# A quarter of the first residual pair on ScalarE's DMA queue, at the front of its program

## The chip, the cores and the metric

One core of a Trainium2 chip. The metric is the device time of one execution in microseconds (us), as a median over fast executions. Profiles are single executions of the same kernels; their span, from first to last instruction, is about 1.8 us shorter than the device time. DMA engines are the 16 engines that move data between memory (HBM) and the core's on-chip memory (SBUF); in these traces a packet is one row of a transfer on one of them (before: 3,072 packets of 16 KB, 128 of the weights' 1,152 bytes, 304 of 4 bytes for the semaphores).

## The reference

A 3x3 convolution with padding 1 over 16 images of 64 channels, 64x64 pixels, plus a residual of the output's shape, all float32:

```python
x        = randn(16, 64, 64, 64)
weight   = randn(64, 64, 3, 3) * 0.1
residual = randn(16, 64, 64, 64)
output[b, co] += weight[co, ci, kh, kw] * x_pad[b, ci, kh:kh+64, kw:kw+64]   # over ci, kh, kw
return output + residual
```

x and residual are read and the output written once: three times 16.8 MB, about 50.5 MB with the weights.

## The kernel before

Images go in pairs: 2 x 64 channels fill the 128 partitions, one image is a row of 4,096 floats (16 KB) per partition. x has three buffers; the residual has one tile `ro` for all eight pairs, into which VectorE adds the convolution from PSUM (TensorE's result memory) and which is then stored. All transfers are issued by SyncE, on one queue, in program order: x pair 0 (moved ahead of the entry barrier, where the engines wait for one another at the start; ScalarE's first recorded instruction comes at 0.96 us), the weights, residual pair 0, x pair 1, residual pair 1, x pair 2, then the rest as buffers come free.

```python
NPIX = H * W                                    # 4096
RES = (slice(0, 1), slice(1, 2), slice(2, 4), slice(4, 6), slice(6, 8))
res_bc = residual.rearrange("(p b) c h w -> (b c) p (h w)", b=2)
...
def load_x(p):
    return nc.sync.dma_start(out=xr[p % NXR][:, :], in_=x_bc[128 * p : 128 * p + 128, :]).then_inc(s_x[p % NXR], 16)

def load_ro(i):
    if i >= 2:
        nc.sync.wait_ge(s_r[i % 2], 16 * (i // 2))
    nc.sync.dma_start(out=ro[:, RES[i], :], in_=res_bc[:, RES[i], :]).then_inc(s_r[i % 2], 16)
...
def to_the_front(dma):       # moves the issue ahead of the first Drain of its engine, before the entry barrier
    ...
for p in range(NPAIR):
    if p >= NXR:
        nc.sync.wait_ge(s_half, 2 * (p - NXR) + 3)
    if p == 0:
        to_the_front(load_x(p))
        nc.sync.dma_start(out=wraw[:, :], in_=w_rows[:, :]).then_inc(s_w, 16)
    else:
        load_x(p)
    if p in (0, 1, 3, 5, 7):
        load_ro((p + 1) // 2)
for k in range(NEARLY):                         # stores of pairs 0-1, 2-3, 4-5; 6 and 7 follow at the end
    nc.sync.wait_ge(s_add, 4 * k + 5)
    store(slice(2 * k, 2 * k + 2)).then_inc(s_out, 16)
```

ScalarE casts x to bfloat16, TensorE transposes the weights once and then runs 384 matmuls, VectorE adds.

Of the kernel before, what the change touches and what calls it, by code (L numbers as in the profile page):

```python
# [15 lines left out]
def kernel(  # L16
# [7 lines left out]
    nc = tc.nc  # L24
# [6 lines left out]
    NPIX = H * W  # L31
# [4 lines left out]
    NXR = 3  # L36
    NXP = 4
    NZERO = 4 + 2 * NXP
    NEARLY = 3
    RES = (slice(0, 1), slice(1, 2), slice(2, 4), slice(4, 6), slice(6, 8))  # L40

    res_bc = residual.rearrange("(p b) c h w -> (b c) p (h w)", b=2)
# [8 lines left out]
    ro = pool.tile([128, NPAIR, NPIX], FP32)  # L51
# [10 lines left out]
    s_r = [sem(f"s_r{i}") for i in range(2)]  # L62
# [8 lines left out]
    def load_x(p):  # L71
        return nc.sync.dma_start(out=xr[p % NXR][:, :], in_=x_bc[128 * p : 128 * p + 128, :]).then_inc(s_x[p % NXR], 16)

    def load_ro(i):
        if i >= 2:
            nc.sync.wait_ge(s_r[i % 2], 16 * (i // 2))
        nc.sync.dma_start(out=ro[:, RES[i], :], in_=res_bc[:, RES[i], :]).then_inc(s_r[i % 2], 16)

    def store(pairs):
        return nc.sync.dma_start(out=out_bc[:, pairs, :], in_=ro[:, pairs, :])  # L80
# [21 lines left out]
    def to_the_front(dma):  # L102



        def fixed(ap):
            t = ap.bass_ap.tensor.name
            return mybir.PhysicalAccessPattern(
                ap=ap.ap, offset=ap.bass_ap.offset, dtype=ap.dtype, memref=t, memsetref=t + "_set", bass_ap=ap.bass_ap
            )  # L110

        front = nc.main_func.blocks[0].instructions
        here = nc.cur_bb.bb.instructions
        ins = here.pop()
        assert ins.name == dma.ins.name
        at = next(
            i for i, e in enumerate(front) if e.engine == ins.engine and isinstance(e, mybir.InstDrain)
        )
        front.insert(at, copy.replace(ins, ins=[fixed(a) for a in ins.ins], outs=[fixed(a) for a in ins.outs]))
# [5 lines left out]
    def weight_block(h, half, d, par, kh):  # L125

        at = 64 * half + 32 * h
        return dict(out=wl[at : at + 32, d, :, par, :], in_=tp[0:32, kh, 0:384].rearrange("p (kw co h) -> p kw co h", kw=3, h=2)[:, :, :, h])

    with tc.tile_critical(no_gpsimd_drain=True):  # L130
# [7 lines that stand above are left out]
                nc.sync.dma_start(out=wraw[:, :], in_=w_rows[:, :]).then_inc(s_w, 16)  # L138
            else:
                load_x(p)  # L140
            if p in (0, 1, 3, 5, 7):
                load_ro((p + 1) // 2)
        for k in range(NEARLY):
            nc.sync.wait_ge(s_add, 4 * k + 5)
            store(slice(2 * k, 2 * k + 2)).then_inc(s_out, 16)


        nc.gpsimd.memset(ident[:, :], 0.0).then_inc(s_id, 1)  # L148
        nc.gpsimd.wait_ge(s_id, 1)
        nc.gpsimd.affine_select(  # L150
            out=ident[:, :],
            in_=ident[:, :],
            compare_op=mybir.AluOpType.not_equal,
            fill=1.0,
            base=0,
            pattern=[[-1, 128]],
            channel_multiplier=1,
        ).then_inc(s_id, 1)
        nc.gpsimd.wait_ge(s_id, 2)
        for t in xp:  # L160
            nc.gpsimd.memset(t[0:64, 0, :], 0.0).then_inc(s_id, 1)  # L161
            nc.gpsimd.memset(t[64:128, J, :], 0.0).then_inc(s_id, 1)  # L162
        nc.gpsimd.memset(wl[0:64, 0, :, 1, :], 0.0).then_inc(s_id, 1)  # L163
        nc.gpsimd.memset(wl[64:128, 1, :, 0, :], 0.0).then_inc(s_id, 1)  # L164


        for n in range(B):
            p, im = divmod(n, 2)
            hp = slice(64 * im, 64 * im + 64)
            x4 = xr[p % NXR].rearrange("q (j two w) -> q j two w", two=2, w=W)  # L170
            t = xp[n % NXP]
            if im == 0:
                nc.scalar.wait_ge(s_x[p % NXR], 16 * (p // NXR + 1))
            i = nc.scalar.copy(out=t[64:128, 0:J, :], in_=x4[hp, :, 0, :])  # L174
            i.then_inc(s_half, 1)
            if n >= NXP:
                i._wait_ge(s_conv, n - NXP + 1)
            nc.scalar.copy(out=t[0:64, 1 : J + 1, :], in_=x4[hp, :, 1, :]).then_inc(s_pack, 1)  # L178
            if n == 0:
                nc.scalar.wait_ge(s_id, NZERO + 1)  # L180
                for b in blocks[4:]:
                    for h in range(2):
                        i = nc.scalar.copy(**weight_block(h, *b))  # L183
                i.then_inc(s_id, 1)


        nc.vector.wait_ge(s_id, NZERO + 1)
        for k, b in enumerate(blocks[:4]):
            for h in range(2):
                i = nc.vector.tensor_copy(**weight_block(h, *b))  # L190
                if k == h == 0:
                    i.then_inc(s_bank, 2)
        i.then_inc(s_id, 1)
        for n in range(B):
            p, im = divmod(n, 2)
            hp = slice(64 * im, 64 * im + 64)
            o4 = ro[:, p, :].rearrange("q (j two w) -> q j two w", two=2, w=W)
            psj = ps[n % 2].rearrange("q c j w -> q (c j) w")
            if im == 0:
                i = next(i for i, pairs in enumerate(RES) if p < pairs.stop)  # L200
                nc.vector.wait_ge(s_r[i % 2], 16 * (i // 2 + 1))
            for par in range(2):
                i = nc.vector.tensor_tensor(  # L203
                    out=o4[hp, :, par, :], in0=psj[64 * par : 64 * par + 64, :, :], in1=o4[hp, :, par, :], op=ADD
                )
                if par == 0:
                    i._wait_ge(s_conv, n + 1)

                i.then_inc(s_add if par == 0 or n == B - 1 else s_bank, 1)


        nc.tensor.wait_ge(s_id, NZERO)
        nc.tensor.wait_ge(s_w, 16)
        wraw3 = wraw.rearrange("p (ci t) -> p ci t", t=9)
        for t in range(9):
            i = nc.tensor.transpose(  # L216
                out=tp[0:32, t // 3, 128 * (t % 3) : 128 * (t % 3) + 128], in_=wraw3[:, :, t], identity=ident[:, :]
            )
        i.then_inc(s_id, 1)
        nc.tensor.wait_ge(s_id, NZERO + 3)  # L220
        with nc.Fori(0, B // NXP, 1, engines=[PE]):
            for n in range(NXP):
                nc.tensor.wait_ge(s_bank, 1).then_inc(s_bank, -1)
                nc.tensor.wait_ge(s_pack, 1).then_inc(s_pack, -1)  # L224
                order = [(1, 0), (1, 1), (0, 0), (0, 1), (2, 0), (2, 1)]
                for i, (kw, d) in enumerate(order):
                    xlo, xhi = max(0, 1 - kw), min(W, W + 1 - kw)
                    for c in range(NCHUNK):
                        j0 = JC * c
                        m = matmul(  # L230
                            ps[n % 2][:, c, :, xlo:xhi],
                            wl[:, d, kw, :, :].rearrange("q r c -> q (r c)"),
                            xp[n][:, j0 + d : j0 + d + JC, xlo + kw - 1 : xhi + kw - 1],
                            i == 0,
                            i == len(order) - 1,
                            c == 0,
                        )
                m.then_inc(s_conv, 1)


    for p in range(2 * NEARLY, NPAIR):
        store(slice(p, p + 1))
    with tc.tile_critical(sync_engine=mybir.EngineType.Pool, no_gpsimd_drain=True):
        nc.gpsimd.wait_ge(s_out, 16 * NEARLY)
        tc.free_semaphores([s_w, *s_x, *s_r, s_out, s_id, s_half, s_pack, s_bank, s_conv, s_add])
# [30 lines left out]
```

## Time and profile before

| | before |
|---|---|
| median time | 122.76 us (3 runs, 122.63 to 122.86) |
| span of the profiled run | 120.8 us |
| first data packet, last data packet | 1.007 us, 119.61 us |
| last addition of VectorE ends | 104.3 us |

### The profile page before, as it was taken

What the parts mean: (1) busy time and instruction counts of PE and PEld (TensorE: products, weight loads), DVE (VectorE), ACT (ScalarE), POOL (GpSimd) and SP (SyncE); (2) the same over time, 40 slices, a digit from 0 to 9 for tenths busy, and PEclk for the clock granted to TensorE, in tenths of its full rate; (3) what the DMA queues carried; (4) which work ended last, traced back from release to release, by engine and by line L of the source; (5) the groups of instructions that cost most, each with busy time, mean ns of one, the idle gap of its engine ahead of it and who ended that gap; (6) DMA issues with size and microseconds to landing.
All of it is one profiled execution on the core that took longest, in us unless ns stands there. A gap on an engine that the chain in (4) does not pass through costs nothing.

```text
span 120.8 us, 734 instructions
## 1 busy us (share of the span) xinstructions
PE 87.9 (73%) x393; PEld 10.7 (9%) x105; DVE 76.0 (63%) x40; ACT 63.1 (52%) x37; POOL 2.4 (2%) x16
## 2 busy tenths in 40 slices
PE   0024499999999999999999999999999990000000
PEld 0011001101010011011111111011111100000000
DVE  0005400789898988989879898988989879500000
ACT  4049959948999923999960999883000000000000
POOL 5200000000000000000000000000000000000000
PEclk9999999999999999999999999999999999855555
DMA  7999999999999999999999999999999999999994
GB/s 168 428 428 428 428 428 434 428 434 434 428 434 434 434 428 434 434 434 434 434 434 423 423 428 434 423 412 434 434 434 434 423 434 434 434 428 434 434 434 174
DMA packets 3504, 50.48 MB, mean 418 GB/s; under 512 B 304, under 2 KB 432, under 8 KB 432
## 3 DMA queue, kind: packets, MB, share of 16 engines
q1 hardware_dynamic: 3504, 50.48, 98.5%
HBM read 33.70 MB, written 16.78 MB: 418 GB/s over the span
## 4 chain that ended last, share of the span: by engine, by line
PE 71%; DVEq 2%; DVE 2%; issue 0%
PE ps L87 53%; PE ps L86 18%; DVEq L130 2%; DVE ro L203 2%
## 5 line engine op out<-in xcount | busy, mean ns | idle before, releaser
L203 DVE TENSOR_TENSOR ro<-ps,ro 64x2048 f32<-64x2048 f32 x32 | 73.2, 2289 | 17.7 <-PE ps L87 17.2
L87 PE MATMUL ps<-xp,wl 128*128 128x504 bf16 (+1 forms) x288 | 80.0, 388 | 0.0
L86 PE MATMUL ps<-xp,wl 128*128 128x504 bf16 (+1 forms) x96 | 37.4, 389 | 3.4 <-PEq L224 3.4
L174 ACT CAST xp<-xr 64x2048 bf16<-64x2048 f32 x16 | 30.3, 1896 | 18.3 <-DMA xr<-in_x_dram 17.2
L178 ACT CAST xp<-xr 64x2048 bf16<-64x2048 f32 x16 | 30.4, 1897 | 0.4
L86 PEld LDWEIGHTS ps<-xp,wl 128*128 128x128 bf16 x96 | 9.5, 99 | 79.1 <-issue 79.1
L190 DVE CAST wl<-ps 32x192 bf16<-32x192 f32 x8 | 2.8, 348 | 10.6 <-PE ps L216 10.5
L216 PE MATMUL ps<-ident,wraw 128*32 128x128 f32 x9 | 2.1, 413 | 8.3 <-DMA wraw<-in_weight_dram 8.3
L216 PEld LDWEIGHTS ps<-ident,wraw 128*32 128x32 f32 x9 | 1.2, 137 | 8.7 <-issue 8.2
L174 ACT ACT_TABLE_LOAD x1 | 1.3, 1283 | 1.0 <-SPq L130 1.0
L183 ACT CAST wl<-ps 32x192 bf16<-32x192 f32 x4 | 1.2, 306 | 0.0
L162 POOL MEMSET xp<- 64x64 bf16 x4 | 0.6, 147 | 0.2
L161 POOL MEMSET xp<- 64x64 bf16 x4 | 0.6, 145 | 0.2
L150 POOL TENSOR_SCALAR_AFFINE_SELECT ident<-ident 128x128 f32<-128x128 f32 x1 | 0.3, 294 | 0.2 <-POOL ident L148 0.2
L164 POOL MEMSET wl<- 64x192 bf16 x1 | 0.3, 253 | 0.1
L163 POOL MEMSET wl<- 64x192 bf16 x1 | 0.3, 252 | 0.1
L148 POOL MEMSET ident<- 128x128 f32 x1 | 0.2, 205 | 0.6 <-SPq L130 0.6
L260 POOL MEMSET const-bfloat16-1.0<- 128x1 bf16 x1 | 0.1, 112 | 0.0
L260 POOL MEMSET const-uint8-127<- 128x1 uint8 x1 | 0.1, 112 | 0.0
L260 POOL MEMSET const-float32-0.0<- 128x1 f32 x1 | 0.1, 105 | 0.2 <-issue 0.2
L260 POOL MEMSET const-float32-1.0<- 128x1 f32 x1 | 0.1, 109 | 0.0
## 6 DMA issues: line engine op xcount, KB each, us to landing
xr<-in_x_dram SPq DMA_DIRECT2D x8, 2048.0 KB, 15.3
ro<-in_residual_dram SPq DMA_DIRECT2D x3, 4096.0 KB, 24.0
out_dram<-ro SPq DMA_DIRECT2D x3, 4096.0 KB, 33.2
ro<-in_residual_dram SPq DMA_DIRECT2D x2, 2048.0 KB, 15.9
out_dram<-ro SPq DMA_DIRECT2D x2, 2048.0 KB, 12.8
wraw<-in_weight_dram SPq DMA_DIRECT2D x1, 144.0 KB, 7.1
```

Of the source, the lines that this page charges most:

```text
L86: return e.matmul(out=out_, lhsT=lhsT, rhs=rhs, start=start, stop=stop, skip_group_check=True)
L87: return e.add_instruction(mybir.InstMatmult(name=nc.get_next_instruction_name(), engine=PE, ins=[e.lower_ap(rhs), e.lower_ap(lhsT)], outs ...
L130: with tc.tile_critical(no_gpsimd_drain=True):
L161: nc.gpsimd.memset(t[0:64, 0, :], 0.0).then_inc(s_id, 1)
L162: nc.gpsimd.memset(t[64:128, J, :], 0.0).then_inc(s_id, 1)
L174: i = nc.scalar.copy(out=t[64:128, 0:J, :], in_=x4[hp, :, 0, :])
L178: nc.scalar.copy(out=t[0:64, 1 : J + 1, :], in_=x4[hp, :, 1, :]).then_inc(s_pack, 1)
L183: i = nc.scalar.copy(**weight_block(h, *b))
L190: i = nc.vector.tensor_copy(**weight_block(h, *b))
L203: i = nc.vector.tensor_tensor(out=o4[hp, :, par, :], in0=psj[64 * par : 64 * par + 64, :, :], in1=o4[hp, :, par, :], op=ADD)
L216: i = nc.tensor.transpose(out=tp[0:32, t // 3, 128 * (t % 3) : 128 * (t % 3) + 128], in_=wraw3[:, :, t], identity=ident[:, :])
L260: nc = _bacc.Bacc("TRN2", target_bir_lowering=False, num_devices=1)
```

## The change

The intent is to use a hole at the very start: SyncE's queue begins slowly (885 KB from 1 to 4 us, where the plateau's rate would give 1,287), so a second queue gets work at once. A quarter of the columns of residual pair 0 (4 KB of each 16 KB row, 0.5 MB) is issued by ScalarE ahead of the entry barrier. SyncE's issue at the old place brings the other 12 KB of each row. The semaphore's counts rise by 16.

```diff
+    R0 = NPIX // 4
...
-    def load_ro(i):
+    def load_ro(i, e=nc.sync, cols=slice(0, NPIX)):
         if i >= 2:
-            nc.sync.wait_ge(s_r[i % 2], 16 * (i // 2))
-        nc.sync.dma_start(out=ro[:, RES[i], :], in_=res_bc[:, RES[i], :]).then_inc(s_r[i % 2], 16)
+            e.wait_ge(s_r[i % 2], 16 * (i // 2 + (i % 2 == 0)))
+        return e.dma_start(out=ro[:, RES[i], cols], in_=res_bc[:, RES[i], cols]).then_inc(s_r[i % 2], 16)
...
-            if p in (0, 1, 3, 5, 7):
+            if p == 0:
+                load_ro(0, cols=slice(R0, NPIX))
+            if p in (1, 3, 5, 7):
                 load_ro((p + 1) // 2)
...
+        to_the_front(load_ro(0, nc.scalar, slice(0, R0)))
...
-                nc.vector.wait_ge(s_r[i % 2], 16 * (i // 2 + 1))
+                nc.vector.wait_ge(s_r[i % 2], 16 * (i // 2 + 1 + (i % 2 == 0)))
```

## The prediction

> **What bounds the kernel now.** I read the page's first parts, then the stretches of the first and last microseconds, then the issues on SyncE's queue. The page:
>
> ```profile
> span 120.8 us, 734 instructions
> PE 87.9 (73%) x393; PEld 10.7 (9%) x105; DVE 76.0 (63%) x40; ACT 63.1 (52%) x37; POOL 2.4 (2%) x16
> ...
> DMA  7999999999999999999999999999999999999994
> GB/s 168 428 428 428 428 428 434 428 434 434 428 434 434 434 428 434 434 434 434 434 434 423 423 428 434 423 412 434 434 434 434 423 434 434 434 428 434 434 434 174
> ...
> q1 hardware_dynamic: 3504, 50.48, 98.5%
> ```
>
> No compute engine is above 73%, while one DMA queue fills the 16 DMA engines for 98.5% of the span, at 423 to 434 GB/s in nearly every slice. The chain that ended last on the page is TensorE's, but it ends with the last addition at 104.3 us; the last 15 us are stores draining. So the bound is the volume, 50.48 MB, and only two things can move the end: fewer DMA idle or slow moments, or cheaper packets. The low slices are the first and the last. The stretches of one microsecond (last two columns: DMA share and GB/s, a packet counted wholly where it starts, so single shares can pass 1):
>
> ```profile
> 0.00:1.00 1.00, 0.00 (x0) 0.00 (x0) 0.00 (x0) 0.04 (x1) 0.22 (x5) 1.00 0.00 0
> 1.00:2.00 1.00, 0.00 (x0) 0.00 (x0) 0.00 (x0) 1.00 (x1) 0.66 (x4) 1.00 1.62 295
> 2.00:3.00 1.00, 0.00 (x0) 0.00 (x0) 0.00 (x0) 0.24 (x1) 0.73 (x6) 1.00 0.58 213
> 3.00:4.00 1.00, 0.00 (x0) 0.00 (x0) 0.00 (x0) 0.00 (x0) 0.78 (x4) 1.00 0.90 377
> 4.00:5.00 1.00, 0.00 (x0) 0.00 (x0) 0.00 (x0) 0.00 (x0) 0.00 (x0) 1.00 1.07 459
> ...
> 118.00:119.00 1.00, 0.00 (x0) 0.00 (x0) 0.00 (x0) 0.00 (x0) 0.00 (x0) 0.50 1.11 475
> 119.00:120.00 1.00, 0.00 (x0) 0.00 (x0) 0.00 (x0) 0.00 (x0) 0.00 (x0) 0.50 0.05 16
> ```
>
> Nothing moves before 1.0 us, and from 1 to 4 us the DMA engines carry 295 + 213 + 377 = 885 KB where about 429 KB per microsecond would be 1,287. The trace's records of single packets say why: the 16 first packets (16 KB each, one per DMA engine) start at 1.007 to 1.275 us and last 0.72 to 2.03 us; the 82 packets that start in the first 5 us average 814 ns, all others 611 ns (the exception is 75 to 80 us, 625 ns, where loads give way to stores). The excess at the start is 82 x (814 - 611) / 16 = 1.04 us per DMA engine. After it there is no idle gap above 20 ns on any DMA engine except one of 121 ns. The last data packet ends at 119.61 us. This 1.04 us is all that a better start can win.
>
> Is the queue ever about to run dry later? SyncE's issues:
>
> ```profile
> 0.00 0.38 SPq L72 DMA_DIRECT2D xr<-in_x_dram  x1
> 1.00 0.33 SPq L138 DMA_DIRECT2D wraw<-in_weight_dram  x1
> 1.38 0.57 SPq L77 DMA_DIRECT2D ro<-in_residual_dram  x1
> 2.00 0.52 SPq L72 DMA_DIRECT2D xr<-in_x_dram  x1
> ...
> 104.58 0.98 SPq L80 DMA_DIRECT2D out_dram<-ro  x2
> ```
>
> Each 2 MB transfer is 8 packets on each of 16 DMA engines, at 607 ns from start to start. Adding up what had been queued, against 2.7 us for the late and slow start and the weights, the queue would have run dry about 7 us after the x load issued at 19.81 us and about 9 us after those issued at 37.31 and 56.78. The closest is the end: before the last two stores were issued at 104.58 us the queue held work until about 119.6 - 16 x 0.607 = 109.9 us, a margin of 5.3 us, or about 4.3 us allowing for the 1.0 us from issue to first packet.
>
> [...]
>
> **The change part by part.** It removes nothing from the volume. The first residual transfer (2 MB, 16 KB rows, issued at 1.38 us behind the weights) becomes two: 0.5 MB in 4 KB rows at ScalarE's front, at about 0.1 us by where ScalarE's first record stands, and 1.5 MB in 12 KB rows at the old place. The semaphore counts rise by 16 to match.
>
> Cost of packets: 16,384 bytes take 607 ns and the weights' 1,152 bytes 47 ns start to start. That is a fixed 4.6 ns and 27.2 bytes per ns. A row of 12 KB plus one of 4 KB is then 456 + 155 = 611 ns, 4.6 more; eight rows per DMA engine give +0.04 us, plus one semaphore write of 9 ns: +0.05 us.
>
> Cost of issuing: ScalarE has an entry barrier to reach, which SyncE reaches at 0.43 us after its own issue of 0.38. An issue of the same length from 0.1 us arrives at about 0.5, so the barrier moves by 0.1 us at most. That moves the weights' issue, which waits behind the first x transfer anyway: 0.
>
> Cost of order: sharing the DMA engines, the first x and the weights land later by up to eight packets of 155 ns, 1.24 us. ScalarE's first cast goes from 7.79 to at most 9.0 us, the transposes from 8.27 to 9.5, TensorE's first conv matmul from 13.78 to at most 15.0. TensorE then runs 86 us without a gap, so the last addition ends at most at 105.5 and the last stores go out at 105.8 instead of 104.58. The margin of 4.3 us absorbs 1.2. The second x load lands where it did, as the bytes ahead of it are the same. Off the path: 0.
>
> Gain: during the slow start each DMA engine now has a second queue. [...] I take one or two residual packets of 155 ns per DMA engine hidden surely (0.15 to 0.3), all of the 1.04 us at best. My estimate is a third to a half of it, -0.4 us. Sum: 122.76 + 0.05 - 0.4 = 122.4 us.
>
> **The rivals.** (A) The slow start is a rate shared by all [...], not a wait of each packet. For: the 16 first packets end one after another, from 1.73 to 3.15 us, as if served in turn. Against: some second packets starting at 2.16 us take the full-speed 611 ns while others beside them still take over 1 us. Then the second queue hides nothing, and the time is 122.76 + 0.05 = 122.8. (B) The slow start is hidden wholly: 122.76 - 1.04 + 0.05 = 121.8[...]. For: 0.5 MB is 1.2 us of work, about the size of the hole. (C) Switching between two queues costs something per packet. [...] Nothing in the profile speaks for it; the change from x rows to weights to residual rows inside one queue costs nothing visible. (D) The later start of TensorE becomes the end: it would need 4.3 us of delay, and at most 1.2 is there. Then 124 or more; I hold it for very unlikely.
>
> **Range and chances.** I give my main path and (B) together about 60%, no effect (A) about 28%, a loss (C, D) about 12%. 122.4 us predicted; 121.7 to 123.0 should hold it 8 times in 10. A gain over 2% needs 2.46 us, more than twice what the start loses, so 0.01 for faster; 0.02 for slower, from unknown costs of a second queue; 0.97 for within 2%.
>
> **What would show it.** Right: a second queue on the page, and 128 more data packets than before; more GB/s between 1 and 4 us than the 885 KB of before; ScalarE's first cast 0.5 to 1.2 us later, TensorE's first conv matmul and the last stores' issue later by about as much, and all the same an earlier last packet (about 119.2 us). No DMA slice below 412 GB/s between the first and the last. Wrong: the last packet at 119.6 or later with the start as slow as before (A), many packets above their size's time in the stretch where both queues are active (C), or a gap of the DMA engines after 105 us (D).

The forecast came to 122.76 + 0.05 - 0.4 = 122.4 us. The gain of -0.4 is the estimate, a third to a half of the 1.04 us that the records of before show; that a second queue hides any of it was not shown at that time. What the trace of before shows: its best slices move 434 GB/s, its first four issues take 0.33 to 0.57 us each, and the first one ends at 0.38 us, 0.62 us before the first packet (1.007 us).

## The result, and the profile after

The changed kernel took 123.14 us (4 runs, 123.05 to 123.31) against 122.81 us for the kernel before (4 runs, 122.63 to 122.95): ratio 1.0029, 95% interval 1.0011 to 1.0047. All ratios here are the mean time of one kernel's fast runs over that of the other's fast runs of the same rounds, so not quite the ratio of the medians. It is slower by 0.33 us, where 0.36 us less than before was predicted; it lies within 2%, but outside the range of 121.7 to 123.0.

The page of the changed kernel, its lines for the DMA:

```profile
span 121.5 us, 735 instructions
...
DMA  6989999999999999999999999999999999999993
GB/s 179 427 335 431 440 431 431 431 431 431 431 431 431 431 431 431 431 431 431 431 431 431 431 431 431 431 431 431 437 426 431 431 426 437 431 431 431 431 431 135
...
q1 hardware_dynamic: 3504, 49.96, 96.9%
q10 hardware_dynamic: 144, 0.52, 1.1%
```

The second queue is there (q10), with 128 data packets and 16 of 4 bytes for the semaphore. The plateau is what it was. What is new is the third slice, 335 GB/s where before had 428. The slices are 3.04 us wide, so that is 6.1 to 9.1 us. The same place in stretches, of the kernel before (last two columns: DMA share and GB/s):

```profile
1.00:5.00 4.00, 0.00 (x0) 0.00 (x0) 0.00 (x0) 1.24 (x1) 2.17 (x12) 1.00 1.04 336
5.00:7.00 2.00, 0.00 (x0) 0.00 (x0) 0.00 (x0) 0.00 (x0) 0.00 (x0) 1.00 0.94 399
7.00:10.00 3.00, 1.73 (x9) 1.16 (x9) 0.00 (x0) 2.18 (x2) 0.00 (x0) 1.00 1.09 460
10.00:14.00 4.00, 0.56 (x3) 0.10 (x1) 2.78 (x8) 3.94 (x6) 0.00 (x0) 1.00 0.99 422
```

and of the changed kernel:

```profile
1.00:5.00 4.00, 0.00 (x0) 0.00 (x0) 0.00 (x0) 1.28 (x1) 2.17 (x12) 1.00 1.02 347
5.00:7.00 2.00, 0.00 (x0) 0.00 (x0) 0.00 (x0) 0.00 (x0) 0.00 (x0) 1.00 0.97 395
7.00:10.00 3.00, 0.00 (x0) 0.00 (x0) 0.00 (x0) 1.10 (x1) 0.00 (x0) 1.00 0.93 352
10.00:14.00 4.00, 2.08 (x9) 1.19 (x9) 1.62 (x5) 3.92 (x7) 0.00 (x0) 1.00 1.05 449
```

From 1 to 5 us the change moves 11 GB/s more for 4 us, 44 KB. From 7 to 14 us it moves 3 x 352 + 4 x 449 = 2,852 KB where before moved 3 x 460 + 4 x 422 = 3,068: 216 KB less, or 0.50 us at 429 KB per us. A packet is counted where it starts, so I take 7 to 14 us together and don't trust the single rows to the last 10%.

The issues and first instructions of the changed kernel, from its timeline:

```profile
0.00 0.38 SPq L73 DMA_DIRECT2D xr<-in_x_dram  x1
0.12 0.36 ACTq L78 DMA_DIRECT2D ro<-in_residual_dram  x1
...
1.07 1.28 ACT L178 ACT_TABLE_LOAD   x1 [1.07 <-SPq L131]
...
8.90 1.90 ACT L178 CAST xp<-xr 64x2048 bf16<-64x2048 f32 x1 [6.54 <-DMA xr<-in_x_dram]
...
10.12 2.08 PE L220 MATMUL ps<-ident,wraw 128*32 128x128 f32 x9 [10.12 <-DMA wraw<-in_weight_dram]
...
15.63 0.58 PE L87 MATMUL ps<-xp,wl 128*128 128x512 bf16 x1 [3.44 <-PEq L228]
...
105.41 0.84 SPq L81 DMA_DIRECT2D out_dram<-ro  x2
```

ScalarE's issue ends at 0.48 us, but by the trace's records of single packets the first packet of its queue starts at 2.95 us; SyncE's first started at 1.04. By 2.95 us the slow start is nearly over: 229 GB/s from 2 to 3 us, 426 from 3 to 4. The last data packet ends at 120.27 us (before: 119.61), with 15 of the 16 DMA engines done by 119.87: one engine lags.

To compare kernels at a glance I added up, from the packet records, the bytes moved by a given time (a packet's bytes spread evenly over its duration) and divided the difference to before by 429.5 KB per us. Plus is ahead of before. All of these kernels move the same bytes; their edits follow below.

| kernel (one trace each) | by 5 us | by 10 us | by 74 us | by 90 us | last packet |
|---|---|---|---|---|---|
| before (KB moved) | 1,217 | 3,356 | 30,964 | 37,820 | 119.61 |
| the change | +0.14 | -0.47 | -0.47 | -0.36 | 120.27 |
| one_queue | -0.10 | -0.44 | -0.44 | -0.33 | 120.50 |
| split_in_place | +0.01 | -0.31 | -0.32 | -0.21 | 120.46 |
| half_act | +0.36 | +0.34 | +0.32 | -0.06 | 119.65 |
| whole_act | +0.38 | +0.43 | +0.38 | -0.06 | 119.82 |
| half_ro4_first | +0.43 | +0.41 | +0.40 | -0.08 | 119.82 |

So the change is ahead a little at 5 us and has lost half a microsecond by 10 us; nothing later adds to the loss.

### The profile page after: what moved, and what is told of

The parts are those of the page before. It is cut to its first block, busy times and chain, and to the rows that moved or that the text cites. A ratio compares the mean times of both kernels' runs of the same rounds, so it can differ in the third digit from the quotient of the medians.

```text
span 121.5 us, 735 instructions
## 1 busy us (share of the span) xinstructions
PE 86.9 (72%) x393; PEld 10.7 (9%) x105; DVE 76.0 (63%) x40; ACT 63.1 (52%) x37; POOL 2.4 (2%) x16
## 3 DMA queue, kind: packets, MB, share of 16 engines
q1 hardware_dynamic: 3504, 49.96, 96.9%
## 4 chain that ended last, share of the span: by engine, by line
PE 70%; DVEq 2%; DVE 2%; issue 0%
PE ps L88 52%; PE ps L87 18%; DVEq L131 2%; DVE ro L207 2%
```

## The experiments

Edits are shown against the changed kernel, unless said otherwise. Theories at the outset: **mixing** (two queues on one DMA engine cost time where their packets alternate), **rows** (rows of 4 KB that lie 16 KB apart in memory are read slowly, whatever the queue), **late TensorE** (the weights land later and the end follows). The first four kernels ran on one chip beside the kernel before at 122.84 us (11 runs, 122.59 to 123.13).

### after_again: the change once more

No edit.

> The changed kernel unchanged, to have its loss beside the others on one chip. All theories: 0.2 to 0.5 us slower than before (ratio 1.001 to 1.004), and the first packet of ScalarE's queue near 2.95 us once more, some 2.5 us after its issue. If that packet comes at about 1.1 us this time, its late start was an accident of one run.

Measured: 123.13 us (6 runs, 122.98 to 123.28), ratio 1.0019 (1.0004 to 1.0033). ScalarE's first packet came at 2.85 us, and the last engine again ended 0.40 us after the next. The loss is small but real, and the late first packet is no accident.

### one_queue: the quarter at the front of SyncE's queue

```diff
                 to_the_front(load_x(p))
+                to_the_front(load_ro(0, nc.sync, slice(0, R0)))
...
-        to_the_front(load_ro(0, nc.scalar, slice(0, R0)))
```

> The same quarter at the front, but of SyncE's queue, right behind the first x transfer: same rows, same early place, one queue. Mixing theory (two queues on one DMA engine cost the time): no packet above its size's time after the slow start, ratio 1.000 to 1.001. Rows theory (4 KB rows at a step of 16 KB are slow to read): the loss stays, ratio about 1.003, with 4 KB packets clearly above 159 ns. Late-TensorE theory: also 1.003, as the weights land late here too.

Measured: 123.51 us (6 runs, 123.26 to 123.63), ratio 1.0049 (1.0034 to 1.0065). There is no second queue, and the loss is twice the change's, also more than the 1.003 that the rows theory forecast. The 4 KB packets took 178 ns on average, up to 394, where 159 is their median in the trace of the change. Mixing falls as the main cause.

### split_in_place: both pieces behind the weights, on SyncE

```diff
             if p == 0:
+                load_ro(0, cols=slice(0, R0))
                 load_ro(0, cols=slice(R0, NPIX))
...
-        to_the_front(load_ro(0, nc.scalar, slice(0, R0)))
```

> SyncE issues both pieces of the first residual pair one after the other at the old place, behind the weights. Mixing theory and late-TensorE theory: as before within 0.1 us (ratio 0.999 to 1.001). Rows theory: ratio about 1.003.

Measured: 123.53 us (6 runs, 123.22 to 123.83), ratio 1.0052 (1.0033 to 1.0070). Here x and the weights land as before and TensorE's first conv matmul starts at 13.99 us (before: 13.78), so late TensorE falls too: cutting the transfer in two, by columns, cost about 0.7 us by itself, where the rows theory had forecast half of that. The 4 KB packets took 190 ns on average.

### whole_act: the whole pair on ScalarE

```diff
-    R0 = NPIX // 4
+    R0 = NPIX
...
-            if p == 0:
-                load_ro(0, cols=slice(R0, NPIX))
```

(The semaphore's counts go back to those of before.)

> ScalarE's front issues the whole first residual pair in 16 KB rows; no extra packets. Mixing theory: packets of both queues alternate up to about 11 us, so the loss is as large as the change's or larger, ratio 1.003 to 1.006. Rows theory: no narrow rows, ratio 1.000. Late-TensorE theory: TensorE starts about 4 us later than the 13.8 us of before, the margin of the last stores is nearly used up, ratio 1.01 or more if that margin is wrong and no loss from it if right.

Measured: 122.84 us (6 runs, 122.68 to 122.93), ratio 0.9995 (0.9981 to 1.0010). No narrow rows, no loss, as the rows theory said, although two queues alternate up to 11.8 us and TensorE starts 4.3 us later than before (18.09 us) with the last stores issued at 107.76 us. Its trace holds a surprise, in two stretches:

```profile
1.00:5.00 4.00, 0.00 (x0) 0.00 (x0) 0.00 (x0) 1.28 (x1) 2.16 (x12) 1.00 1.02 385
...
78.00:82.00 4.00, 4.00 (x20) 0.49 (x5) 3.50 (x2) 2.72 (x2) 0.00 (x0) 1.00 0.99 369
```

The kernel before, in the later of the two stretches (in the earlier it moved 336 GB/s):

```profile
78.00:82.00 4.00, 4.00 (x21) 0.43 (x5) 3.39 (x3) 3.19 (x3) 0.00 (x0) 1.00 1.00 418
```

The second queue does fill a part of the hole at the start: 49 GB/s more for 4 us, some 0.4 us of work. And the gain is given back near 79 us, where the loads end and the stores begin. There the records show 31 packets above 650 ns in this kernel, up to 1,242, nearly all of them loads; before has 9, the change and the two kernels above have none. (These counts, like all of single packets here, are from the trace's packet records, one trace each.)

The next four ran on one chip beside before at 122.88 us (9 runs, 122.73 to 123.09).

### rows_act: the quarter cut by partitions

```diff
-    R0 = NPIX // 4
+    R0 = 32
...
-        return e.dma_start(out=ro[:, RES[i], cols], in_=res_bc[:, RES[i], cols]).then_inc(s_r[i % 2], 16)
+        return e.dma_start(out=ro[rows, RES[i], :], in_=res_bc[rows, RES[i], :]).then_inc(s_r[i % 2], 16)
```

(ScalarE takes partitions 0 to 31, SyncE 32 to 127.)

> The same quarter of bytes at ScalarE's front, but cut by partitions: 32 whole rows of 16 KB, the other 96 on SyncE. Rows theory (the loss is the 4 KB rows at a step of 16 KB): no loss, and the better start is kept, 0.2 to 0.4 us faster than before, ratio 0.997 to 0.999, no DMA engine more than 0.3 us behind the next at the end. Mixing theory: a loss as in the change, ratio 1.002 to 1.004.

Measured: 127.18 us (5 runs, 127.09 to 127.51), ratio 1.0351 (1.0337 to 1.0365). Both theories missed. Its stretches, with ScalarE's 32 partitions in flight in the first row and SyncE's 96 in the second:

```profile
3.00:7.00 4.00, 0.00 (x0) 0.00 (x0) 0.00 (x0) 0.00 (x0) 0.85 (x5) 1.00 0.99 254
10.00:16.00 6.00, 2.08 (x9) 1.16 (x9) 2.76 (x8) 5.64 (x7) 0.00 (x0) 1.00 1.00 227
```

The DMA engines are busy all the time (0.99 and 1.00) but move little over half of the usual 430 GB/s: in the second stretch most 16 KB packets take 1.1 to 1.25 us instead of 0.61. Why, no run shows. What is shown is that the rate is little over half while a transfer of 32 partitions (beside x's packets) or one of 96 (alone) is in flight, so this kernel could not test the rows theory.

### extra_step16, extra_contig, extra_step20: the suspected read by itself

The kernel before, with one more load of 128 rows of 4 KB into a tile that nobody reads (GpSimd waits for it at the very end). Queue, place, sizes and destination are the same in all three; only the addresses in memory differ.

```diff
+    extra = nc.alloc_sbuf_tensor("extra", [128, 1024], FP32)
+    extra_src = res_bc[:, 0, 0:1024]                     # extra_step16: rows 16 KB apart
+    extra_src = <residual, flat>[0 : 128 * 1024]         # extra_contig: one after the other, as (128, 1024)
+    extra_src = <residual, flat> as (128, 5 * 1024)[:, 0:1024]    # extra_step20: rows 20 KB apart
...
                 nc.sync.dma_start(out=wraw[:, :], in_=w_rows[:, :]).then_inc(s_w, 16)
+                nc.sync.dma_start(out=extra[:, :], in_=extra_src).then_inc(s_extra, 16)
```

> Before, with one more load of 128 rows of 4 KB into a tile nobody reads, behind the weights; the rows lie 16 KB apart in memory. The volume alone costs 8 x 0.155 = 1.24 us, so 124.1. Every form of the rows theory: 0.4 to 0.6 more, ratio 1.013 to 1.016.

> The same with the 128 rows of 4 KB one after the other in memory. If the step in memory is the cause: 124.1 us, ratio 1.010, every 4 KB packet at about 159 ns. If a run of short packets is the cause wherever they read [...]: as with the step of 16 KB, ratio 1.013 to 1.016, with 4 KB packets of 200 ns and more.

> The same with the rows 20 KB apart. If what is slow is that all rows share one place modulo 16 KB: as the contiguous one, ratio 1.010. If any gap between rows is slow: as the step of 16 KB. If short packets are slow: all three alike.

Measured, 4 runs each: step 16 KB 124.44 us (124.35 to 124.56), ratio 1.0123; contiguous 124.31 us (124.13 to 124.37), ratio 1.0112; step 20 KB 124.20 us (124.08 to 124.26), ratio 1.0105. The 95% intervals are about 0.0015 to either side and overlap, so the times alone decide little; the contiguous load also cost 0.2 us more than I expected, and the step of 16 KB cost 0.13 to 0.24 us more than the other two where 0.4 to 0.6 was forecast. The packets decide. With one queue, the packets of each DMA engine follow one another (in before, after the slow start, with no gap above 20 ns); chained to eight 4 KB rows on each of the 16 engines, with the least idle time between them, they give the time that each engine spends on its rows:

| eight 4 KB rows, ns per DMA engine | least | median | most |
|---|---|---|---|
| extra_contig (16 engines) | 1,248 | 1,248 | 1,249 |
| extra_step20 (16) | 1,248 | 1,248 | 1,249 |
| extra_step16 (16) | 1,248 | 1,322 | 1,684 |
| one_queue (16) | 1,248 | 1,354 | 1,750 |
| split_in_place (16) | 1,317 | 1,480 | 1,859 |

The stretch of 7 to 10 us says the same on the page's own scale. The contiguous load:

```profile
7.00:10.00 3.00, 1.55 (x8) 1.11 (x9) 0.00 (x0) 1.98 (x2) 0.00 (x0) 1.00 1.10 456
```

The step of 16 KB:

```profile
7.00:10.00 3.00, 1.57 (x8) 1.16 (x9) 0.00 (x0) 2.02 (x2) 0.00 (x0) 1.00 1.05 402
```

Short packets in a row were not slow (1,248 ns for eight, contiguous), nor were gaps (1,248 at 20 KB): of the three loads of 4 KB rows only the one with the step of 16 KB was (median 1,322), where every row starts at the same place modulo 16 KB. Why these rows were slower, no run shows. The size is partly open: the step costs 0.13 to 0.24 us here, while split_in_place lost 0.7. In split_in_place the rows are slower on average (1,516 ns against 1,365) and the worst engine loses 0.61 us; why the same addresses are slower there, I don't know.

That worst engine is the one that ends last, and its packets can be followed from end to end. In split_in_place it is done with x at 7.63 us, with its residual rows at 13.53, and ends at 120.46; the last engine of before is done with x at 7.42, with the same bytes at 12.67, and ends at 119.61. From there both need 106.9 us. So in these two traces the whole 0.85 us was lost by 13.5 us: 0.20 in a later x, 0.61 in the 4 KB rows, and 0.05, which is what the prediction had reckoned for the cut.

The third group ran beside before at 122.81 us (9 runs; one at 143.56 counts as slow and is left out).

### extra_act_contig and extra_act_step16: the same read on ScalarE's front

```diff
-                nc.sync.dma_start(out=extra[:, :], in_=extra_src).then_inc(s_extra, 16)
...
+        to_the_front(nc.scalar.dma_start(out=extra[:, :], in_=extra_src).then_inc(s_extra, 16))
```

> The extra load of 128 rows of 4 KB, contiguous in memory, moved from SyncE behind the weights to ScalarE's front. If a second queue by itself costs time (mixing theory): above the 124.3 us that the same load cost on SyncE's queue. If the second queue wins a part of the slow start and only the step in memory costs: 123.9 to 124.2 us, ratio 1.008 to 1.010, and a cumulative count of bytes that is 0.15 to 0.4 us ahead of before from 5 us on, after allowing for the volume.

> The same at ScalarE's front with the rows 16 KB apart. Step theory: 0.1 to 0.3 us above the contiguous one at ScalarE's front, as on SyncE's queue (124.44 against 124.31). If mixing is what costs: no difference between the two.

Measured: contiguous 123.99 us (5 runs, 123.91 to 124.11), ratio 1.0103; step of 16 KB 124.11 us (4 runs, 124.05 to 124.16), ratio 1.0108. Against the same loads on SyncE's queue (124.31 and 124.44, measured in the group before, on another chip) both are about 0.3 us faster; allowing for the kernel before on each chip that is some 0.25 us by the medians and 0.11 and 0.18 by the ratios, within their intervals. So no net cost of mixing is seen, and the gain is not clear of the noise; the step costs 0.12 again, within the intervals, with 4 KB packets of 168 ns on average against 161. By 5 us the contiguous one had moved 129 KB more than before, 0.30 us.

### half_act: half of the columns

```diff
-    R0 = NPIX // 4
+    R0 = NPIX // 2
```

> Half of the columns at ScalarE's front instead of a quarter: both pieces have rows of 8 KB at a step of 16 KB. Step theory: both pieces now read only half of each 16 KB[...], and the gain of the start is larger; ratio 1.000 to 1.003. Mixing theory: packets alternate for longer, ratio above 1.004.

Measured: 122.77 us (5 runs, 122.66 to 122.92), ratio 1.0004 (0.9990 to 1.0018). Rows of 8 KB at the same step were not slow: 310 ns on average, 332 at most, on average 26.4 bytes per ns against the 26.8 of a 16 KB row in 611 ns. Its start is 0.36 us ahead, and in 78 to 82 us it moves 385 GB/s against the 418 of before: the gain is given back as in whole_act.

### whole_act_again: is the late loss an accident?

No edit to whole_act.

> The whole pair at ScalarE's front once more. Its first trace was 0.38 us ahead of before from 5 us on and lost 0.5 us where loads give way to stores, near 79 us. If that loss belongs to the kernel it comes again and the ratio is 1.000 (0.999 to 1.001); if it was an accident of that run, the ratio is 0.996 to 0.998.

Measured: 122.94 us (5 runs, 122.87 to 122.99), ratio 1.0016 (1.0002 to 1.0030). The ratio is a little above the range forecast for either case. The second trace again is 0.41 us ahead at 74 us and 0.06 behind at 90 us; another slow patch near 110 us puts it 0.3 behind. The loss near 79 us belongs to the kernel, the second patch to this trace alone.

The last four ran on the chip of the third group, beside before at 122.79 us (its runs and one more; the slow one left out).

### swap and act_late: why ScalarE's first packet is late

swap exchanges the two issues at the front; act_late leaves out the move to the front.

```diff
+                to_the_front(load_ro(0, nc.sync, slice(0, R0)))       # swap
-                to_the_front(load_x(p))
...
+        to_the_front(load_x(0, nc.scalar))                           # swap
+        load_ro(0, nc.scalar, slice(0, R0))                          # act_late
-        to_the_front(load_ro(0, nc.scalar, slice(0, R0)))            # both
```

> The first x transfer goes to ScalarE's front and the quarter to SyncE's front. In the changed kernel the first packet of ScalarE's queue comes 2.3 to 2.5 us after its issue ends, SyncE's 0.6 us after. If the lateness belongs to ScalarE's queue, the first x packets now come at about 2.8 us, the DMA engines have only the quarter to do until then, and the time is 0.5 us or more above the change's: 123.6 and more. If it belongs to whichever issue comes second, x starts near 1.1 us, the quarter near 2.9, and the time is the change's 123.1.

> The quarter is issued by ScalarE after the entry barrier, at about 1.0 us, instead of at its front. If the first packet of ScalarE's queue comes a fixed 2.4 us after the issue, it now comes near 3.8 us, after the slow start, the start gains nothing and the time is that of the one-queue versions less little: 123.3 to 123.5. If it comes near 2.9 us whatever the issue time, the time is the change's 123.1.

Measured: swap 123.41 us (4 runs, 123.34 to 123.43), ratio 1.0051 (1.0035 to 1.0067); act_late 123.40 us (123.23, 123.40 and 123.71; a fourth at 145.2 is left out as slow), ratio 1.0045 (1.0026 to 1.0064). In swap, ScalarE's queue carries x, issued at 0.12 us, and its first packet starts at 2.65 us, while SyncE's quarter starts at 1.00. In act_late, the issue is

```profile
0.96 0.39 ACTq L78 DMA_DIRECT2D ro<-in_residual_dram  x1
```

and the first packet comes at 4.96 us, 3.6 us after that line ends. The time of swap lies between its two forecasts (123.6 and 123.1), and the first packet of act_late later than either of its own (3.8 and 2.9 us). So in these runs ScalarE's queue starts late whatever it carries, and not by a fixed time: from the end of its issue 2.4 to 2.5 us in the change and its repetition, 2.2 in swap, 3.6 in act_late, against SyncE's 0.62 in before. My swap was not clean, though: ScalarE's issue still is the second one in time, so "the second to issue" isn't excluded as the cause.

### half_ro4_first and before_ro4_first: what is slow near 79 us

```diff
+            if p == 7:
+                load_ro(4)
             if p >= NXR:
...
-            if p in (1, 3, 5, 7):
+            if p in (1, 3, 5):
```

(On half_act; the control has the same two lines on the kernel before.)

> The version with half of the columns on ScalarE, with the last residual load put ahead of the last x load, so that other loads stand last before the stores. Its trace was 0.37 us ahead of before from 5 us on and lost 0.45 us in slow loads at 78 to 80 us. If those slow loads belong to the residual rows, they go and the kernel keeps the gain: 122.4 us, ratio 0.996 to 0.998. If they belong to the turn from loads to stores whatever is loaded, x loads are slow in their place and the ratio stays at 1.000.

> The kernel before with the same exchange, as the control: it lost only 0.1 us at that place, so both theories say 122.7 to 122.9, ratio 0.998 to 1.001.

Measured: half_ro4_first 122.92 us (5 runs, 122.75 to 122.98), ratio 1.0012 (0.9998 to 1.0026); the control 122.95 us (6 runs, 122.79 to 123.30), ratio 1.0022 (1.0005 to 1.0040). The control was a little slower than expected, for a reason I haven't found. In half_ro4_first:

```profile
1.00:5.00 4.00, 0.00 (x0) 0.00 (x0) 0.00 (x0) 1.28 (x1) 2.16 (x12) 1.00 1.01 377
78.00:82.00 4.00, 4.00 (x20) 0.49 (x5) 3.39 (x3) 0.69 (x1) 0.00 (x0) 1.00 1.00 373
```

Ahead at the start, slow before the stores, as without the exchange, although the packets that are slow are now loads of x. The residual rows are not the cause: 78 to 82 us has 385 GB/s without the exchange (half_act) and 373 with it. The slow stretch is at the turn from loads to stores, in the kernels that come to it early: the change and the kernels with the cut on one queue, which come to it 0.3 us and more behind before, show no slow packet there (418 GB/s in the change, 438 in one_queue and split_in_place). The loads of the extra rows fit: extra_act_contig, 0.28 us ahead, has 20 packets above 650 ns at its turn, extra_contig and extra_step20, level with before, 3 and 5. And the kernels that come early all leave at the same point, 0.06 to 0.08 us behind before, whether they were 0.32 or 0.40 ahead. That is a pattern of one trace each; why an early arrival is slowed I could not settle.

## Why the prediction was wrong

**The bound: right.** Both kernels are bound by the DMA engines, whose queues fill 98.5% of the span in before and 96.9 + 1.1% in the change; no compute engine changed its busy time by more than about 1 us, and whole_act shows that even a TensorE start 4.3 us later leaves the time alone (ratio 0.9995).

**The cost of packets: the step that failed.** The prediction says: "A row of 12 KB plus one of 4 KB is then 456 + 155 = 611 ns, 4.6 more; eight rows per DMA engine give +0.04 us, plus one semaphore write of 9 ns: +0.05 us." That line was drawn through packets of transfers whose rows follow one another in memory without gaps. split_in_place makes this cut and nothing else and lost 0.69 us (123.53 against 122.84); one_queue, with the narrow rows early, lost 0.67. The 12 KB rows were at fault in neither (460 and 462 ns on average, where the median in the change is 460); the 4 KB rows were, at 178 and 190 ns on average against 159. That packets at the step of 16 KB were slower is shown by extra_step16 (median 1,322 ns for eight) against extra_contig and extra_step20 (1,248). In the trace of split_in_place the slowed rows of the last engine make 0.61 of its 0.85 us; why they cost more there than in extra_step16 stays open. Part of the loss is that the slowed rows are spread unevenly: the end waits for the last DMA engine, which in the change ends 0.40 us after the next, while in before the last two are 0.02 us apart.

**The gain: right in kind, too large here.** The estimate was -0.4 us. By 5 us the change is ahead by 0.14 in bytes moved (44 KB, or 0.10 us, in the stretches). The prediction took for granted that ScalarE's packets would be there while the start is slow; they came at 2.95 us, when it was nearly over. From 1 to 4 us it moved 966 KB against 885, so the sign that the prediction named for a gain was there. With larger or contiguous packets on ScalarE the gain by 5 us was 0.30 to 0.43 us, as estimated. So in those kernels a second queue won what was hoped by then, but the quarter of 4 KB rows didn't collect it, and no version kept it to the end.

**The sum** was 122.76 + 0.05 - 0.4 = 122.4. With the measured terms it is +0.69 for the cut, taken from split_in_place, and about -0.36 for going to ScalarE's front, which is only the difference left to the measured +0.33; the packet records don't split it so neatly, since by 10 us the change and one_queue are equally far behind (0.47 and 0.44 us) and differ in their last engine (120.27 against 120.50).

**Issue and order: nearly right.** The barrier moved by 0.11 us (the table load from 0.96 to 1.07 us; predicted 0.1 at most). The first cast came at 8.90 (at most 9.0 predicted). The weights came later than predicted: transposes at 10.12 instead of at most 9.5, the first conv matmul at 15.63 instead of 15.0; the weights' small packets took up to 326 ns, against 51 in before, beside the slowed rows. The last stores' issue moved only to 105.41 (at most 105.8). None of it is on the path.

**The rivals.** (A), a start that a second queue can't speed up, is not what happened: other versions are ahead at 5 us, though none in its time. (B), the hole filled wholly, is shown by none: the most was 0.43 of the 1.04 us, the size of the main estimate, and it was lost at the turn, which no rival had. (C), a price per packet of two queues, has the right sign and the wrong cause: without a second queue the loss is larger. (D), late TensorE, never came near.

**Smaller errors.** In (B) the prediction gave the ends of single DMA engines as 118.8 to 119.6 us; the lower figure took in packets before the last, and it is 119.1 to 119.6. The one idle gap of 121 ns that it puts after the slow start lies inside it, at 1.86 us. And its checks for "wrong" looked for a start "as slow as before" or slow packets where two queues are active; the sign that spoke was one that it had listed under "right", no slice below 412 GB/s: the third fell from 428 to 335.

No version tried beats the kernel before: the best, whole_act (ratio 0.9995) and half_act (1.0004), are level with it.

## What to carry to other kernels

Don't cut a transfer by columns as if a packet's cost depended on its length alone: rows of 4 KB at a step of 16 KB were slower here (eight of them took a median of 1,322 ns per DMA engine) than such rows end to end or 20 KB apart (1,248), and cutting by partitions was far worse (127.18 us). Here the end was that of the last DMA engine, in the change 0.40 us after the next, so look at how far the engines are apart and not only at their mean. And follow a gain at the start through to the end: here 0.4 us were there at 74 us and gone at 90 (whole_act: +0.38 and -0.06).
